# A hybrid S5 / HGRN2 / gated-MLP block in fp32: another order of the first twelve weight steps, and the S5 column work on GpSimd

## The chip, the cores and the metric

The kernel runs on one core of one Trainium2 chip. The metric is the device time of one execution in microseconds (us). Before the change it is 1422.86 us, the median of three runs (1422.52 to 1424.83). Lower is better.

## The reference

One block of a decoder in float32 on a sequence of 256 tokens with 2048 channels. `x` is normalised, multiplied by a wide input matrix, split into an S5 branch, an HGRN2 branch and two gates, merged, multiplied by an output matrix, added to `x`, and put through a gated MLP with a short causal convolution and a final norm.

```python
h = _rmsnorm(x, ln_mix_g[l])
proj = h @ w_in[l]                                  # 2048 x 9216
u_s5, q_h, f_h, i_h, g_h, gate_s5, gate_hgrn = jnp.split(proj, _in_splits(), axis=-1)
y_s5 = _s5_branch(u_s5, ...) @ w_proj_s5[l]
y_hgrn = _hgrn2_branch(q_h, f_h, i_h, g_h, lb_all[l], hgrn_norm_g[l]) @ w_proj_hgrn[l]
merged = sigmoid(gate_s5) * y_s5 + sigmoid(gate_hgrn) * y_hgrn
x = x + merged @ w_out[l]
x = x + _conv_glu_ffn(_rmsnorm(x, ln_ffn_g[l]), w_up[l], conv_w[l], conv_b[l], w_down[l])
# inside _s5_branch, per group g and state p (64 x 64 pairs):
dt = exp(log_dt)[:, None]; mag = exp(lam_re * dt)
abar_re = mag * cos(lam_im * dt); abar_im = mag * sin(lam_im * dt)
den = lam_re * lam_re + lam_im * lam_im
coef_re = ((abar_re - 1) * lam_re + abar_im * lam_im) / den
coef_im = (abar_im * lam_re - (abar_re - 1) * lam_im) / den
```

## The kernel before, in words

**Weight steps.** All weights are read once, in pieces of 128 x 1024 floats (512 KB). A piece is a step: SyncE's queue loads it into `wr` (four buffers), ScalarE (ACT) rounds it to `wh` (fp32r), VectorE (DVE) makes the rest `wl = wr - wh`, both with three buffers, and TensorE (PE) multiplies: for the feature-major jobs of the front (`fm_job`, wide) 8 matmuls of 512 columns with `wh` (against the high and the low half of x at once) and 8 of 256 columns with `wl`. A job is a block of 256 output columns: four steps (g = 0 to 3, one for each 512 rows of `w_in`) that add up in one PSUM bank, then an epilogue. The loop at the end of the kernel loads five steps ahead (`LOAD_AHEAD`) and splits two ahead (`LA`). Step i can run only when chunk g of x is ready: `x_chunk(g)` transposes 512 columns of x on PE (eight 128 x 128 transposes into `ax`), ACT writes the high half of `hT`, DVE the low half.

**The front.** Here jobs run one after the other: the first job (`u_jobs[0]`, four steps) needs all four chunks of x, and `between` puts `x_chunk(i+1)` between the two parts of step i. `warm_up` runs matmuls of `ones` into `dummy`. `x_norm` (sum of squares on DVE, then `rstd_of`, then `broadcast_rows` through PE) and `x_params` (a transpose of parameter rows to `colA`) follow at step 2. The epilogue `epi_u` of a job waits for the row `R_x` that `x_norm` makes.

**The sides.** `side_s5` and `side_hgrn` are generators that are advanced a few yields after each step (`side_run`), whenever the counted DVE load isn't ahead of PE's. The first part of `side_s5` is column work: parameters transposed to `colB` and `colC`, then some 110 small DVE operations on 128 x 32 or 128 x 16 floats (`exp_parts` for dt, for mag and for the softmax of the HGRN lower bound; a range reduction of the angle; the coefficients). Then come tables of angles (`tabA`, `tabB`), `BB` (coefficients times B), `X` (C placed by group, then transposed), and from there per channel tile `angle_sum` on GpSimd (128 x 1024), `b_place` into `zmat`, projections and scans.

**What sets the order.** The code gives an order, but a scheduler under it places each engine's instructions, and may put a later one ahead where it takes an engine for free; `tc.issue_after` (`behind_x`) keeps some from being put too early. Inside `tc.manual_schedule` (used by the changed kernel) the named engines keep the order of the code for what is written there; instructions written behind that block may still be placed between those of the block.

Of the kernel before, what the change touches and what calls it, by code (L numbers as in the profile page):

```python
# [110 lines left out]
def kernel(  # L111
# [28 lines left out]
    WARM_H = 6  # L140
    NORM_AT = 2
# [35 lines left out]
    ones = cst.tile([P, P], F32, name="ones")  # L177
    G.memset(ones, 1.0)
    epsc = cst.tile([P, 1], F32, name="epsc")
    G.memset(epsc, EPS)  # L180
# [17 lines left out]
    S.dma_start(out=packG, in_=rows(ln_mix_g))  # L198
    G.memset(packA, 0.0)
    ldt = pack[0:64, 5 * P:5 * P + 2]  # L200

    def load_params():
        S.dma_start(out=packA[16:32, :], in_=rows(lb_logits))
        S.dma_start(out=packA[56:72, :], in_=rows(ln_ffn_g))
        S.dma_start(out=packA[72:104, :], in_=a_re.rearrange("o (q g) p -> (o q) (g p)", g=2))
        S.dma_start(out=packB[0:32, :], in_=a_im.rearrange("o (q g) p -> (o q) (g p)", g=2))

# [63 lines left out]
    def fm_job(wap, c0, nkc, xs, epi, need=None, extra_load=None, wide=False):  # L271
# [121 lines left out]
    def x_chunk(g, between=None):  # L393

        for h in range(2):
            if h == 1 and between is not None:
                between()
# [5 lines left out]
            for a in range(2):  # L403
                kc = 4 * g + 2 * h + a
                A.activation(out=hT[:, kc, 0, :], in_=ax[:, a * T:(a + 1) * T], func=AF.Copy, scale=g_mix[:, kc:kc + 1])  # L405
# [5 lines left out]
        box["x"] = [getattr(i, "ins", i) for i in (last, lastp)]  # L411

    @contextmanager
    def behind_x():

        with tc.issue_after(box["x"][0]), tc.issue_after(box["x"][1]):
            yield

    def x_first():
        ax = axbank()  # L420
        PE.transpose(ax[:, 0:16], packG, ident[:16, :16])
        V.tensor_copy(g_mix, ax[:, 0:16])
        x_chunk(0, lambda: split_step(steps[0]))
        with behind_x():
            warm_up(WARM_H, ones)

    def x_norm():
        ss = cst.tile([P, 2, 4], F32, name="ss_x")
        for g in range(4):
            for j in range(2):  # L430
                xc = x_tok[j][g // 2][:, (g % 2) * 512:(g % 2) * 512 + 512]
                junk = tmp()
                V.scalar_tensor_tensor(out=junk, in0=xc, scalar=1.0, in1=xc, op0=ALU.mult, op1=ALU.mult,
                                       accum_out=ss[:, j, g:g + 1])
# [3 lines left out]
        broadcast_rows(R_x, r_x)  # L438
# [92 lines left out]
    u_jobs = [fm_job(w_in, 256 * p, 16, xs_hw, epi_u(p), wide=True) for p in range(4)]  # L531
# [25 lines left out]

    def exp_parts(new, xin):
# [6 lines left out]
        V.tensor_scalar(out=xc, in0=xin, scalar1=-88.0, scalar2=88.3, op0=ALU.max, op1=ALU.min)  # L565
        V.tensor_scalar(out=n, in0=xc, scalar1=1.4426950408889634, scalar2=ROUND, op0=ALU.mult, op1=ALU.add)
        V.tensor_scalar(out=n, in0=n, scalar1=-ROUND, scalar2=None, op0=ALU.add)
        V.scalar_tensor_tensor(out=r, in0=n, scalar=-0.693359375, in1=xc, op0=ALU.mult, op1=ALU.add)
        V.scalar_tensor_tensor(out=r, in0=n, scalar=2.12194440e-4, in1=r, op0=ALU.mult, op1=ALU.add)
        V.tensor_scalar(out=t, in0=r, scalar1=1.9875691500e-4, scalar2=1.3981999507e-3, op0=ALU.mult, op1=ALU.add)  # L570
        for c in (8.3334519073e-3, 4.1665795894e-2, 1.6666665459e-1, 5.0000001201e-1):
            V.tensor_tensor(out=t, in0=t, in1=r, op=ALU.mult)
            V.tensor_scalar(out=t, in0=t, scalar1=c, scalar2=None, op0=ALU.add)
        V.tensor_tensor(out=t, in0=t, in1=r, op=ALU.mult)
        V.tensor_tensor(out=t, in0=t, in1=r, op=ALU.mult)
        V.tensor_tensor(out=e, in0=t, in1=r, op=ALU.add)
        V.tensor_scalar(out=si, in0=n, scalar1=127.0, scalar2=8388608.0, op0=ALU.add, op1=ALU.mult)
        return e, si.bitcast(F32)

    def side_s5():  # L580
# [56 lines left out]
        V.tensor_scalar(out=t1, in0=th, scalar1=4097.0, scalar2=None, op0=ALU.mult)  # L637
        V.tensor_tensor(out=thh, in0=t1, in1=th, op=ALU.subtract)
        V.tensor_tensor(out=thh, in0=t1, in1=thh, op=ALU.subtract)
        V.tensor_tensor(out=thl, in0=th, in1=thh, op=ALU.subtract)  # L640
        for i, (src, c) in enumerate(((thh, c1), (thh, c2), (thl, c1))):
            V.tensor_scalar(out=ph, in0=src, scalar1=c, scalar2=None, op0=ALU.mult)
            V.tensor_scalar(out=pr, in0=ph, scalar1=ROUND, scalar2=ROUND, op0=ALU.add, op1=ALU.subtract)
            V.tensor_tensor(out=ph, in0=ph, in1=pr, op=ALU.subtract)
            V.tensor_scalar(out=pr, in0=ph, scalar1=ROUND12, scalar2=ROUND12, op0=ALU.add, op1=ALU.subtract)
            if i == 0:
                V.tensor_copy(hi, pr)
                V.tensor_tensor(out=lo, in0=ph, in1=pr, op=ALU.subtract)
            else:
                V.tensor_tensor(out=hi, in0=hi, in1=pr, op=ALU.add)  # L650
                V.tensor_tensor(out=ph, in0=ph, in1=pr, op=ALU.subtract)
                V.tensor_tensor(out=lo, in0=lo, in1=ph, op=ALU.add)
        V.scalar_tensor_tensor(out=lo, in0=thl, scalar=c2, in1=lo, op0=ALU.mult, op1=ALU.add)
        V.scalar_tensor_tensor(out=lo, in0=th, scalar=c3, in1=lo, op0=ALU.mult, op1=ALU.add)
        V.tensor_scalar(out=pr, in0=hi, scalar1=ROUND, scalar2=ROUND, op0=ALU.add, op1=ALU.subtract)
        V.tensor_tensor(out=hi, in0=hi, in1=pr, op=ALU.subtract)
# [3 lines left out]
        V.tensor_tensor(out=ph, in0=hi, in1=lo, op=ALU.add)  # L660
        V.tensor_scalar(out=pr, in0=ph, scalar1=-0.5, scalar2=0.5, op0=ALU.max, op1=ALU.min)
# [742 lines left out]
```

## Time and profile before

| | us |
|---|---|
| median of the runs shown | 1422.86 |
| the profiled execution's own time | 1422.75 |
| its span (first to last instruction) | 1420.6 |
| PE busy | 1403.4 |
| DVE busy | 1056.9 |
| ACT busy | 757.7 |
| GpSimd (POOL) busy | 38.0 |

In the timeline a row reads: start in us, length in us, engine, line, operation, tiles out<-in, shape, count, and in brackets how long the engine stood idle before it and what it waited for. Nearly every operation of PE and DVE goes through a metering helper, so it bears line L106; tiles tell them apart. A length can overlap the next start: the pace of PE is read from start to start. `PEld` are weight loads of PE, `SPq`, `ACTq` and `POOL DMA` rows are the issue of transfers.

### The profile page before, as it was taken

How to read it: one execution, taken by the hardware profiler on the slowest of the kernel's cores; microseconds unless marked ns; L12 is line 12 of the kernel's file. 1: busy time of each engine (PE TensorE's matmuls, PEld its weight loads, DVE VectorE, ACT ScalarE, POOL GpSimd, SP SyncE). 2: the span in 40 equal slices, each digit the busy share in tenths (PEclk: the TensorE clock that was granted, in tenths of full speed). 3: DMA queues.
4: the chain of work that ended last, by engine and by line, in shares of the span. 5: the costliest groups of instructions: out<-in, count | busy, mean ns of one | idle time of the engine just before them, and what ended most of it. 6: DMA issues, size and time to landing. Idle time of an engine off the chain costs nothing.

```text
span 1420.6 us, 20722 instructions
## 1 busy us (share of the span) xinstructions
PE 1403.4 (99%) x8008; PEld 1182.1 (83%) x8008; DVE 1056.9 (74%) x1453; ACT 757.7 (53%) x962; POOL 38.0 (3%) x33
## 2 busy tenths in 40 slices
PE   9999999999999999999999999999999999999997
PEld 7878887877778787888888888888888888888885
DVE  7999989998978968655777777777777775545454
ACT  5455576665655464454555555555555554434343
POOL 1040000000001000000000000000000000000000
PEclk9999999999999999999999999999999999999999
DMA  7865767666767466666666666666666666666653
GB/s 237 219 195 149 218 206 219 202 205 187 210 191 262 154 199 207 220 212 207 193 191 185 188 192 187 186 191 191 185 189 191 188 187 193 201 193 201 194 194 125
DMA packets 215940, 278.58 MB, mean 196 GB/s; under 512 B 19938, under 2 KB 141042, under 8 KB 215841
## 3 DMA queue, kind: packets, MB, share of 16 engines
q1 hardware_dynamic: 198496, 266.57, 60.5%
q10 hardware_dynamic: 17088, 10.49, 2.4%
q8 instruction: 63, 1.03, 0.3%
q14 instruction: 37, 0.30, 0.1%
q0 software_dynamic: 256, 0.19, 0.0%
HBM read 266.73 MB, written 10.49 MB: 195 GB/s over the span
## 4 chain that ended last, share of the span: by engine, by line
PE 95%; DVE 2%; DMA 1%; ACT 1%; issue 0%; POOL 0%; ACTq 0%; DVEq 0%; POOLq 0%
PE mm L106 87%; PE ax L106 7%; DVE u L106 1%; PE bu L106 1%; DMA u<-d 1%; DVE wl L106 1%; DMA u<-in_s_log_dt_dram 0%; ACT wh L256 0%; DVE t L106 0%; PE dummy L106 0%; DVE zmat L106 0%; ACT u L1275 0%; DVE x2g L106 0%; ACT hT L405 0%; ACT t L1259 0%
## 5 line engine op out<-in xcount | busy, mean ns | idle before, releaser
L256 ACT CAST wh<-wr 128x1024 fp32r<-128x1024 f32 x480 | 503.0, 1051 | 587.7 <-PE mm L106 424.2
L106 DVE TENSOR_TENSOR wl<-wr,wh 128x1024 fp32r<-128x1024 f32 x480 | 588.2, 1228 | 304.3 <-ACT wh L256 301.3
L106 PE MATMUL mm<-x2g,wh 128*128 128x512 f32 x1408 | 352.6, 392 | 0.0
L106 PEld LDWEIGHTS mm<-x2g,wh 128*128 128x128 f32 x1408 | 253.3, 189 | 45.3
L106 PE MATMUL mm<-wh,u 128*128 128x512 f32 x1040 | 260.7, 392 | 0.0
L106 PEld LDWEIGHTS mm<-wh,u 128*128 128x128 f32 x1040 | 193.7, 188 | 39.7
L106 PEld LDWEIGHTS mm<-x2g,wl 128*128 128x128 f32 x1408 | 192.0, 190 | 13.6
L106 PE MATMUL mm<-x2g,wl 128*128 128x256 f32 x1408 | 196.4, 282 | 0.0
L106 PE MATMUL mm<-wh,hT 128*128 128x512 f32 x768 | 193.6, 394 | 0.0
L106 PEld LDWEIGHTS mm<-wh,hT 128*128 128x128 f32 x768 | 142.1, 188 | 33.5 <-issue 2.9
L106 PE MATMUL mm<-wl,u 128*128 128x512 f32 x520 | 140.6, 390 | 0.0
L106 DVE TENSOR_TENSOR u<-u,u 128x512 f32<-128x512 f32 (+4 forms) x144 | 114.8, 821 | 0.5
L106 PEld LDWEIGHTS mm<-wl,u 128*128 128x128 f32 x520 | 97.4, 188 | 20.0
L106 PE MATMUL mm<-wl,hT 128*128 128x512 f32 x384 | 102.9, 390 | 0.0
L106 PE MATMUL mm<-hT,wh 128*128 128x512 f32 x384 | 100.4, 401 | 0.8 <-ACT wh L256 0.8
L106 PEld LDWEIGHTS mm<-wl,hT 128*128 128x128 f32 x384 | 72.1, 188 | 15.5
L106 PEld LDWEIGHTS mm<-hT,wh 128*128 128x128 f32 x384 | 69.9, 192 | 14.8 <-ACT wh L256 1.0
L106 DVE SCALAR_TENSOR_TENSOR t<-ub,colC,t 128x256 f32<-128x256 f32 x176 | 73.3, 479 | 0.0
L106 PEld LDWEIGHTS mm<-hT,wl 128*128 128x128 f32 x384 | 52.1, 191 | 4.7 <-DVE wl L106 1.3
L106 PE MATMUL mm<-hT,wl 128*128 128x256 f32 x384 | 54.3, 284 | 0.3 <-DVE wl L106 0.3
L1200 ACT ACTIVATE t<-ub,colC 128x256 f32<-128x256 f32 x88 | 48.0, 593 | 0.0
L106 PE MATMUL ax<-wh,u 128*128 128x512 f32 x176 | 43.3, 389 | 0.0
(186 smaller groups left out, 861.2 us busy)
## 6 DMA issues: line engine op xcount, KB each, us to landing
wr<-in_w_up_dram SPq DMA_DIRECT2D x176, 512.0 KB, 4.5
wr<-in_w_in_dram SPq DMA_DIRECT2D x144, 512.0 KB, 4.4
wr<-in_w_down_dram SPq DMA_DIRECT2D x88, 512.0 KB, 4.7
wr<-in_w_out_dram SPq DMA_DIRECT2D x32, 512.0 KB, 4.2
wr<-in_w_proj_s_dram SPq DMA_DIRECT2D x16, 512.0 KB, 4.0
wr<-in_w_proj_hgrn_dram SPq DMA_DIRECT2D x16, 512.0 KB, 4.8
d<-t ACTq DMA_DIRECT2D x28, 256.0 KB, 4.4
rl<-d SPq DMA_DIRECT2D x16, 256.0 KB, 4.3
```

The costliest lines, as they stand in the source:

```text
L106: return fn(*args, **kw)
L256: A.copy(st.wh, st.w)
L1200: A.activation(out=av, in_=ub[:, a, 0:T], func=AF.Identity, scale=conv_col(0, n), bias=colC[:, 264 + n:265 + n])
```

## The change

It reorders the front: the first three jobs go chunk by chunk (`FRONT = 3`; steps 0, 1, 2 use chunk 0 of x, steps 3, 4, 5 chunk 1, and so on; the third job gets the PSUM bank `bu`, named `mf` here), under a hand-written order for SyncE, PE, ACT and DVE. The first weight piece and the first chunk of x come in halves on two queues. Squares of x go from DVE to ACT. The S5 column work goes from DVE to GpSimd (`E = G`; a fused multiply-add becomes two instructions), the softmax part behind `BB`. Four parameter loads go from SyncE's queue to GpSimd's. The diff, cut:

```diff
-    WARM_H = 6
-    NORM_AT = 2
+    WARM_H = 3
+    FRONT = 3
...
-    G.memset(ones, 1.0)
+    V.memset(ones, 1.0)
...
-    S.dma_start(out=cf, in_=cst_f)
+    A.dma_start(out=cf, in_=cst_f)
...
-    def load_params():
-        S.dma_start(out=packA[16:32, :], in_=rows(lb_logits))
...
+    G.dma_start(out=packA[72:104, :], in_=a_re.rearrange("o (q g) p -> (o q) (g p)", g=2))
+    G.dma_start(out=packB[0:32, :], in_=a_im.rearrange("o (q g) p -> (o q) (g p)", g=2))
+    G.dma_start(out=packA[16:32, :], in_=rows(lb_logits))
+    G.dma_start(out=packA[56:72, :], in_=rows(ln_ffn_g))
...
+                if fine and g == 0:
+                    for h, part in ((0, 0), (0, 1), (0, 2), (1, 0), (1, 1), (1, 2)):
+                        for k in (2 * h, 2 * h + 1):
+                            for j in range(2):
...
+                                PE.matmul(o, (wl if part == 2 else wh)[:, k, cols], hT[:, k, part % 2, :],
+                                          start=k == 0 and part == 0, stop=False)
+                    return
...
+    def load_first():
...
+        for h in range(2):
+            for j in range(2):
+                S.dma_start(out=x_tok[j][0][:, h * T:(h + 1) * T], in_=x[0, j * P:(j + 1) * P, h * T:(h + 1) * T])
+            st.dma = A.dma_start(out=v3(st.w, 4)[:, 2 * h:2 * h + 2, :], in_=st.src[:, 2 * h:2 * h + 2, :])
...
+    def x_squares(g):
+        for j in range(2):
...
+            A.activation(out=junk, in_=xc, func=AF.Square, accum_out=ss_x[:, j, g:g + 1])
...
+    steps[:4 * FRONT] = [steps[4 * p + g] for g in range(4) for p in range(FRONT)]
...
+    E = G
+    def fused(out, in0, scalar, in1, op0, op1, t):
+        E.tensor_scalar(out=t, in0=in0, scalar1=scalar, scalar2=None, op0=op0)
+        E.tensor_tensor(out=out, in0=t, in1=in1, op=op1)
...
+        yield ("step", 9)
         A.activation(out=sn, in_=pr, func=AF.Sin, scale=TWO_PI)
...
+        E.tensor_tensor(out=den, in0=den, in1=t1, op=ALU.add)
...
+        yield ("step", 11)
+        V.reciprocal(out=den, in_=den)
+        E.tensor_tensor(out=cr, in0=nr, in1=lam_re, op=ALU.mult)
...
+        yield ("step", 18)
+        V.reciprocal(out=e1, in_=e0)
...
+    with tc.manual_schedule(engines={ET.SP, ET.PE, ET.Activation, ET.DVE}):
+        load_first()
+        table_up()
+        for i in range(1, LOAD_AHEAD):
+            load_front(i)
+        warm_up(WARM, ones)
+        x_first()
+        for i in range(4 * FRONT):
+            g, r = divmod(i, FRONT)
+            load_front(i + LOAD_AHEAD)
+            if r == FRONT - 1 and g < 3:
+                x_chunk(g + 1)
+            split_step(steps[i + 1])
...
+            work(i, steps[i])
+            if i == 3 * FRONT - 1:
+                x_norm()
+            elif i == 3 * FRONT + 1:
+                broadcast_rows(R_x, r_x)
+            if i == 2:
+                x_params()
+            if i >= 2:
...
+                side_run()
```

How it moves instructions, at three places. First PE at the start of the program, before the change (`ax` are transposes, `u_88` to `u_91` the tiles of x, `mm_225` the bank of the first job, `wh_196` and `wl_197` the two parts of step 0, `wh_215` of step 1, `wh_221` of step 2):

```order
L106 MATMUL dummy<-ones 128x128 x6
L106 MATMUL ax_234<-cf,u_88 128x128
L106 MATMUL mm_225<-hT,wh_196 128x512 x8
...
L106 MATMUL mm_225<-hT,wl_197 128x256 x8
L106 MATMUL mm_225<-hT,wh_215 128x512 x2
L106 MATMUL ax_274<-cf,u_89 128x128
...
L106 MATMUL mm_225<-hT,wl_216 128x256 x8
```

The same place after the change (`u_90` to `u_93` are now x; `mm_226`, `mm_259` and `mf_304` the banks of the first three jobs, `u_78` the parameter rows):

```order
L106 MATMUL dummy<-ones 128x128 x3
L106 MATMUL mm_226<-hT,wh_186 128x256 x8
L106 MATMUL mm_226<-hT,wl_187 128x256 x4
...
L106 MATMUL mm_259<-hT,wh_218 128x512 x8
L106 MATMUL mm_259<-hT,wl_219 128x256 x8
...
L106 MATMUL mf_304<-hT,wl_256 128x256 x8
L106 MATMUL ax_321<-cf,u_78 128x104
L106 MATMUL ax_331<-cf,u_78 128x64
L106 MATMUL ax_334<-cf,u_78 128x128 x2
L106 MATMUL ax_334<-cf,u_78 128x96
L106 MATMUL mm_226<-hT,wh_296 128x512 x8
```

Chunk 1 of x was needed right after step 0 and is now needed after step 2; the parameter transposes moved from steps 7 and 8 to the place between steps 2 and 3.

Second, DVE behind the split of step 3 (`wl_297`), after the change; `wl_368` and `wl_449` are the splits of steps 4 and 5, `u_413` holds small S5 columns, here `den`, and the brackets name the semaphore that a row waits for:

```order
L106 TENSOR_TENSOR wl_297<-wr_175,wh_296 128x1024 [waits DMAHW4_49,Activation_49]
L106 COPY colA<-ax_321 128x104 [waits PE_49]
L106 COPY u_78<-u_78 32x128 [waits DMASW7_49]
L106 COPY colB<-ax_331 128x64 [waits PE_49]
L106 COPY colC<-ax_334 128x352 [waits PE_49]
L106 RECIPROCAL u_413<-u_413 128x32 [waits Pool_49]
L106 TENSOR_TENSOR wl_368<-wr_177,wh_367 128x1024 [waits DMAHW5_49,Activation_49]
L106 TENSOR_TENSOR wl_449<-wr_216,wh_448 128x1024 [waits DMAHW6_49,Activation_49]
```

The reciprocal of `den` is written behind step 11, and stands behind the split of step 3, ahead of the splits of steps 4 and 5; before the change no DVE row of the front waits for GpSimd.

Third, GpSimd at the start of the column work, after the change (`u_339` and `u_413` hold the columns):

```order
L655 TENSOR_SCALAR u_339<-colA 128x32 [waits DVE_49]
L616 TENSOR_SCALAR u_339<-colB 128x32 [waits DVE_49]
L706 TENSOR_TENSOR u_413<-u_339 128x32 [waits Pool_49]
L617 TENSOR_SCALAR u_339<-u_339 128x32 [waits Pool_49]
L618 TENSOR_SCALAR u_339<-u_339 128x32 [waits Pool_49]
...
L678 TENSOR_SCALAR u_413<-u_413 128x32 [waits Pool_49]
L708 TENSOR_TENSOR u_413<-u_413 128x32 [waits Pool_49]
```

These rows stood on DVE before; the last one makes `den`. From the row that reads `colB` to that last row there are 40 instructions, and nearly all of them wait for an earlier one of the same engine.

More of the change, by code (lines that the diff above doesn't have):

```diff
@@ L174, in at, with rows @@
             return self.units[k // 4][:, (k % 4) * T:(k % 4 + n) * T]
+    pack = unit()
+    packA, packB = pack[0:104, 0:P], pack[0:64, P:2 * P]
+    packC = [pack[0:P if i < 2 else 96, (2 + i) * P:(3 + i) * P] for i in range(3)]
+    def rows(ap):
+        return ap.rearrange("o (r c) -> (o r) c", c=P)
+    packG = pack[0:16, 6 * P:7 * P]
+    S.dma_start(out=packG, in_=rows(ln_mix_g))
     ones = cst.tile([P, P], F32, name="ones")
-    G.memset(ones, 1.0)
+    V.memset(ones, 1.0)
     epsc = cst.tile([P, 1], F32, name="epsc")
@@ L410, in x_chunk @@
                                               op0=ALU.mult, op1=ALU.subtract)
-        box["x"] = [getattr(i, "ins", i) for i in (last, lastp)]
+        box["x"] = [getattr(i, "ins", i) for i in (last, lastp, lasta)]
     @contextmanager
     def behind_x():
-        with tc.issue_after(box["x"][0]), tc.issue_after(box["x"][1]):
+        with tc.issue_after(box["x"][0]), tc.issue_after(box["x"][1]), tc.issue_after(box["x"][2]):
             yield
     def x_first():
+        st = steps[0]
+        uid[0] += 1
+        st.wh = wp.tile([P, 1024], F32R, tag="wh", name=f"wh{uid[0]}", bufs=LA + 1)
+        st.wl = wp.tile([P, 1024], F32R, tag="wl", name=f"wl{uid[0]}", bufs=LA + 1)
         ax = axbank()
@@ L422, in x_first @@
         V.tensor_copy(g_mix, ax[:, 0:16])
-        x_chunk(0, lambda: split_step(steps[0]))
-        with behind_x():
-            warm_up(WARM_H, ones)
-    def x_norm():
[L428 to L434, printed above, removed]
+        for h in range(2):
+            ax = axbank()
+            half = slice(h * 512, h * 512 + 512)
+            A.copy(st.wh[:, half], st.w[:, half])
+            for a in range(2):
+                for j in range(2):
+                    c = (2 * h + a) * P
+                    PE.transpose(ax[:, a * T + j * P:a * T + (j + 1) * P], x_tok[j][0][:, c:c + P], ident)
+            for a in range(2):
+                kc = 2 * h + a
+                xa, gk = ax[:, a * T:(a + 1) * T], g_mix[:, kc:kc + 1]
+                if kc == 0:
+                    V.tensor_scalar(out=hT[:, kc, 0, :], in0=xa, scalar1=gk, scalar2=None, op0=ALU.mult)
+                else:
+                    A.activation(out=hT[:, kc, 0, :], in_=xa, func=AF.Copy, scale=gk)
+            for a in range(2):
+                kc = 2 * h + a
+                V.scalar_tensor_tensor(out=hT[:, kc, 1, :], in0=ax[:, a * T:(a + 1) * T], scalar=g_mix[:, kc:kc + 1],
+                                       in1=hT[:, kc, 0, :].bitcast(F32), op0=ALU.mult, op1=ALU.subtract)
+            V.tensor_tensor(out=st.wl[:, half], in0=st.w[:, half], in1=st.wh[:, half].bitcast(F32), op=ALU.subtract)
+        warm_up(WARM_H, ones)
+    ss_x = cst.tile([P, 2, 4], F32, name="ss_x")
+    def x_squares(g):
+        for j in range(2):
+            xc = x_tok[j][g // 2][:, (g % 2) * 512:(g % 2) * 512 + 512]
+            junk = tmp()
+            A.activation(out=junk, in_=xc, func=AF.Square, accum_out=ss_x[:, j, g:g + 1])
+    def x_norm():
+        ss = ss_x
         ssum = cst.tile([P, 2], F32, name="ssum_x")
@@ L529, with front_bank @@
     gh_dram = [[scratch() for _ in range(2)] for _ in range(4)]
-    u_jobs = [fm_job(w_in, 256 * p, 16, xs_hw, epi_u(p), wide=True) for p in range(4)]
+    def front_bank():
+        uid[0] += 1
+        return psb.tile([P, 2, 512], F32, tag="bu", name=f"mf{uid[0]}")
+    u_jobs = [fm_job(w_in, 256 * p, 16, xs_hw, epi_u(p), wide=True, bank=front_bank if p == 2 else mm_bank, fine=p == 0)
+              for p in range(4)]
+    steps[:4 * FRONT] = [steps[4 * p + g] for g in range(4) for p in range(FRONT)]
     for p in range(4):
@@ L685, in side_s5 @@
+        fused(nr, cm1, 1.0, em1, ALU.add, ALU.mult, nr)
+        E.tensor_tensor(out=nr, in0=nr, in1=cm1, op=ALU.add)
+        E.tensor_tensor(out=ni, in0=mag_c, in1=sn, op=ALU.mult)
+        E.tensor_tensor(out=den, in0=lam_re, in1=lam_re, op=ALU.mult)
+        E.tensor_tensor(out=t1, in0=lam_im, in1=lam_im, op=ALU.mult)
+        E.tensor_tensor(out=den, in0=den, in1=t1, op=ALU.add)
         AB = unit()
@@ L695, in side_s5 @@
             yield
+        yield ("step", 11)
+        V.reciprocal(out=den, in_=den)
+        E.tensor_tensor(out=cr, in0=nr, in1=lam_re, op=ALU.mult)
+        E.tensor_tensor(out=t1, in0=ni, in1=lam_im, op=ALU.mult)
+        E.tensor_tensor(out=cr, in0=cr, in1=t1, op=ALU.add)
+        E.tensor_tensor(out=cr, in0=cr, in1=den, op=ALU.mult)
+        E.tensor_tensor(out=ci, in0=ni, in1=lam_re, op=ALU.mult)
+        E.tensor_tensor(out=t1, in0=nr, in1=lam_im, op=ALU.mult)
+        E.tensor_tensor(out=ci, in0=ci, in1=t1, op=ALU.subtract)
+        E.tensor_tensor(out=ci, in0=ci, in1=den, op=ALU.mult)
+        yield ("step", 12)
         BB = unit()
@@ L876, in side_hgrn @@
         mraw = reload_tile()
-        S.dma_start(out=mraw[:, 0:112], in_=cst_m)
-        V.tensor_copy(masks, v3(mraw[:, 0:80], 5))
+        with behind_x(), tc.issue_after(getattr(steps[4 * FRONT].dma, "ins", steps[4 * FRONT].dma)):
+            S.dma_start(out=mraw[:, 0:112], in_=cst_m)
+            V.tensor_copy(masks, v3(mraw[:, 0:80], 5))
         q, k, f = (Chunks(8) for _ in range(3))
@@ L1326, in side_run, with load_front, work @@
                     return
-    for i in range(LOAD_AHEAD):
-        if i < 4:
-            load_x_chunk(i)
+    def load_front(i):
+        if i % FRONT == 0 and i < 4 * FRONT:
+            load_x_chunk(i // FRONT)
         load_step(steps[i])
-        if i == 4:
-            load_params()
-    table_up()
-    warm_up(WARM, ones)
-    x_first()
-    for i in range(1, LA):
-        split_step(steps[i])
-    for i in range(3):
-        steps[i].between = lambda i=i: x_chunk(i + 1)
-    load["dve"] = load["pe"] = 0.0
-    for i, st in enumerate(steps):
-        if i + LOAD_AHEAD < len(steps):
-            load_step(steps[i + LOAD_AHEAD])
-        if i + LA < len(steps):
-            split_step(steps[i + LA])
+    def work(i, st):
         run_later(i=i)
@@ L1356 @@
             st.extra_load()
+        fin.add(("step", i))
         st.mm(st)
-        if i == NORM_AT:
-            with behind_x():
-                x_norm()
-                x_params()
         if st.after is not None:
             job, fn = st.after
-            later.append((i + 1, job, fn))
-        load["dve"] = max(load["dve"], load["pe"] - 4.0)
-        if i >= S5_START:
-            pauses[0] = 0
-            if i == S5_START:
-                with behind_x():
-                    side_run()
-            else:
-                side_run()
+            later.append((i + (2 if i < 4 * FRONT else 1), job, fn))
+    ET = mybir.EngineType
+    with tc.manual_schedule(engines={ET.SP, ET.PE, ET.Activation, ET.DVE}):
+        load["dve"] = load["pe"] = 0.0
+        load_first()
[10 more added lines that the diff above has]
+            split_step(steps[i + 1])
+            if i == 0:
+                x_squares(0)
+            elif r == FRONT - 1 and g < 3:
+                x_squares(g + 1)
+            work(i, steps[i])
[6 more added lines that the diff above has]
+            if i >= 2:
+                pauses[0] = 0
+                load["dve"] = max(load["dve"], load["pe"] - 4.0)
+                side_run()
+    for i in range(1, LA):
+        split_step(steps[4 * FRONT + i])
+    for i, st in enumerate(steps):
+        if i < 4 * FRONT:
+            continue
+        if i + LOAD_AHEAD < len(steps):
+            load_front(i + LOAD_AHEAD)
+        if i + LA < len(steps):
+            split_step(steps[i + LA])
+        work(i, st)
+        load["dve"] = max(load["dve"], load["pe"] - 4.0)
+        pauses[0] = 0
+        side_run()
     run_later(i=len(steps) + 10)
```

157 lines of the change are left out of this document (65 added, 92 removed).

## The prediction

> **What bounds the kernel now.** The page first: span, busy times and the chain that ended last; then who waited for whom on PE.
>
> ```profile
> span 1420.6 us, 20722 instructions
> PE 1403.4 (99%) x8008; PEld 1182.1 (83%) x8008; DVE 1056.9 (74%) x1453; ACT 757.7 (53%) x962; POOL 38.0 (3%) x33
> PE 95%; DVE 2%; DMA 1%; ACT 1%; issue 0%; POOL 0%; ACTq 0%; DVEq 0%; POOLq 0%
> PE ax L106 <- DVE u L106: 3.3, 2, 2.3
> PE ax L106 <- DMA u<-in_x_dram: 1.1, 1, 1.1
> PE mm L106 <- ACT wh L256: 0.8, 1, 0.8
> ```
>
> PE is busy for 99% and is 95% of the chain. The change takes no matmul away, so it can only win what PE loses, and PE's waits are a few us in all. Everything is therefore decided by when PE starts on weights, and by the few places of the first 110 us where it stands. The timeline of PE and DVE shows both.
>
> ```profile
> 1.00 3.36 PE L106 MATMUL dummy<-ones 128*128 128x128 f32 x14 [1.00 <-POOL epsc L180]
> 5.67 0.48 PE L106 MATMUL ax<-cf,u 128*128 128x128 f32 x1 [1.10 <-DMA u<-in_x_dram]
> 8.26 2.43 PE L106 MATMUL dummy<-ones 128*128 128x128 f32 x12
> 10.56 1.62 PE L106 MATMUL mm<-hT,wh 128*128 128x512 f32 x6
> 47.07 2.12 PE L106 MATMUL mm<-hT,wh 128*128 128x512 f32 x8 [0.78 <-ACT wh L256]
> 49.97 2.00 PE L106 MATMUL mm<-hT,wh 128*128 128x512 f32 x8
> 51.81 1.12 PE L106 MATMUL mm<-hT,wl 128*128 128x256 f32 x8
> 52.77 2.00 PE L106 MATMUL mm<-hT,wh 128*128 128x512 f32 x8
> 95.34 1.03 PE L106 MATMUL ax<-cf,u 128*128 128x128 f32 x8
> 96.14 2.09 PE L106 MATMUL mm<-hT,wh 128*128 128x512 f32 x8
> 101.50 1.14 PE L106 MATMUL ax<-cf,u 128*128 128x128 f32 x8 [2.33 <-DVE u L106]
> 102.32 3.67 PE L106 MATMUL mm<-hT,wh 128*128 128x512 f32 x8
> 102.00:106.00 4.00, 4.00 (x16) 3.29 (x14) 2.41 (x3) 2.66 (x4) 0.00 (x0) 0.57 0.75 222
> ```
>
> Weights start at 10.56. A step takes 2.80 us (49.97 to 52.77): 1.84 for the wide part, 0.96 for the rest. Steps 0 to 11 fill 10.56 to 49.97, 39.4 us: twelve times 2.80 is 33.6, the 24 transposes of chunks 1 to 3 are 2.4 (eight take 0.80, from 95.34 to 96.14), and parameter and broadcast matmuls about 1.6 (below); so only 1.8 us are waits. The other loss is at 99 to 106: 2.33 us idle, and then eight wide matmuls in 3.67 instead of 2.00, since the granted clock is 0.57 in that window. That is 4.0 us together.
>
> **The change part by part. Start.** Two rows of the windows (the last number is GB/s):
>
> ```profile
> 0.00:5.00 5.00, 3.57 (x15) 3.24 (x15) 0.15 (x1) 1.49 (x2) 4.25 (x16) 1.00 0.37 100
> 5.00:10.00 5.00, 4.03 (x17) 3.45 (x18) 1.89 (x6) 2.14 (x5) 1.20 (x6) 1.00 0.98 335
> ```
>
> 0.5 MB is in by 5 us and then 0.335 MB per us. I keep that curve: the first halves of x and of weight piece 0 with the constants are 0.6 MB, in at 5.3; the second halves end at 1.1 MB, 6.8 us. Then come four transposes and three dummies of two passes, all at the early pace of about 0.21 us (14 passes in 3.36, 12 in 2.43): 0.85 and 1.3, so weights start near 9.0 instead of 10.56: **-1.55**. PE runs at the slow pace until about 10 (the 12 passes from 8.26), so step 0 gets **+0.5**, and 24 narrow matmuls of 0.12 instead of 8 wide and 8 narrow are **+0.1**. Pieces 1 and 2 (1.6 and 2.2 MB: 8.3 and 10) and chunk 1 (2.7 MB, 11.5) come before PE wants them, since three steps per chunk are 8.4 us of PE work; the waits of 1.8 go: **-1.8**. The moved loads cost nothing: SyncE's queue has four issues less, and GpSimd's twelve at some 0.5 us are out by 8 us, ten before `ax_321`. Squares on ACT (eight) lie beside a PE step each; ACT is 53% busy. What covers them is the two steps by which splits run ahead.
>
> **Parameters.** PE now does these three transposes in a row, and the second waits for two DVE copies.
>
> ```profile
> 36.03 0.63 PE L106 MATMUL ax<-dg,ones 128*128 128x128 f32 x4
> 36.51 0.28 PE L106 MATMUL ax<-cf,u 104*128 104x104 f32 x1
> 37.87 0.46 PE L106 MATMUL ax<-cf,u 128*128 128x128 f32 x3
> 37.04 0.26 DVE L106 COPY colA<-ax 128x104 f32<-128x104 f32 x1
> 5.70 0.45 DVE L106 COPY u<-u 32x128 f32<-32x128 f32 x1 [3.27 <-DMA u<-in_s_log_dt_dram]
> ```
>
> 0.26 and 0.45 less some overlap: **+0.6**. The front without the reciprocal is then -1.55 + 0.5 + 0.1 - 1.8 + 0.6 = **-2.1**.
>
> **The reciprocal on DVE.** In the new order DVE takes `den`'s reciprocal ahead of the split of step 4, and `den` is the end of 40 GpSimd instructions that begin when `colB` is copied. Behind the waiting reciprocal stand the splits of steps 4 and 5 and the low halves of chunk 2, and PE waits for the first. From the copy of `colB` PE still has the last parameter transposes (0.5), step 3 (2.80) and the wide part of step 4 (1.84), together 5.1. DVE needs the copy and hand-over (0.4), 40 GpSimd instructions of c each, the reciprocal (0.34), the split (1.22) and hand-overs (0.2). PE stands 40c - 3.0. No row shows c: GpSimd did no small arithmetic before. The nearest rows:
>
> ```profile
> L180 POOL MEMSET epsc<- 128x1 f32 x1 | 0.1, 99 | 0.0
> L732 POOL MEMSET zmat<- 128x256 f32 x1 | 0.3, 331 | 0.0
> L741 POOL TENSOR_TENSOR u<-u x8: 1942/2544/7529, 77.8 to 285.3; 128x1024 f32<-128x1024 f32 x8
> 1413.52 0.16 DVE L106 TENSOR_TENSOR fin<-fin 128x1 f32<-128x1 f32 x1
> 1413.71 0.16 DVE L106 TENSOR_TENSOR fin<-fin,fin 128x1 f32<-128x1 f32 x1
> 57.74 0.34 DVE L106 RECIPROCAL u<-u 128x32 f32<-128x32 f32 x1
> L106 DVE TENSOR_TENSOR wl<-wr,wh 128x1024 fp32r<-128x1024 f32 x480 | 588.2, 1228 | 304.3 <-ACT wh L256 301.3
> ```
>
> The memsets give 0.10 + 0.0009 per element: 0.13 for 32, the low end, as nothing is read there. On DVE a chain in which each waits for the last advances by 0.19 (1413.52 to 1413.71). From above: if the sum of 1024 elements in 1.94 to 2.1 us spends two thirds to all of its time on elements, 0 to 0.7 is fixed; half of that, 0.35, plus a wait gives 0.40 as high end. I take **0.25**: nearer in size to the memsets, in kind to the sums, and above DVE's 0.19. 40c is then 10.0 (5.2 to 16), and PE stands **+7.0** (2.2 to 13). PE idle for 2.33 us was followed by the half clock, so **+1.7** again. After it DVE has 1.2 to 1.8 us of work per PE step of 2.8 and catches up. ACT's two sines wait for the 84th of these instructions; at c = 0.25 that is 21 us after `colB`, beside steps 4 to 9 and the stall.
>
> **Later.** The 4.0 us at 99 to 106 came from DVE running late:
>
> ```profile
> 77.83 11.68 POOL L741 TENSOR_TENSOR u<-u 128x1024 f32<-128x1024 f32 x3 [71.63 <-DVE u L106]
> 82.88 0.68 DVE L106 TENSOR_TENSOR u<-u,u 128x512 f32<-128x512 f32 x1
> 83.48 4.25 DVE L106 TENSOR_SCALAR u<-u,cf 128x512 f32<-128x512 f32 x2
> 95.32 5.24 DVE L106 TENSOR_TENSOR wl<-wr,wh 128x1024 fp32r<-128x1024 f32 x3 [0.59 <-ACT wh L256]
> 100.48 0.87 DVE L106 TENSOR_SCALAR u<-u,cf 128x512 f32<-128x512 f32 x2
> L106 DVE TENSOR_TENSOR u<-u 128x32 f32<-128x32 f32 x34 | 5.7, 185 | 0.1
> L106 DVE TENSOR_SCALAR u<-u 128x32 f32<-128x32 f32 x28 | 4.8, 176 | 0.1
> ```
>
> Two scalings took 4.25 beside GpSimd's sums, and 0.87 alone. Some 100 small operations leave DVE (the last two rows, of 40 to 72 us: 62 of them take 10.5 us), which speaks for no gap; a second reciprocal, of 8 columns, waits for 25 GpSimd instructions, and the sums still run beside the same scalings, which speaks for one. I take half back: **-2.0** (-4.0 to +4.0).
>
> By the Trainium skill's "SBUF — State Buffer", SBUF: two separate sides, DVE with two SBUF inputs and GpSimd exclude each other on a shared port pair; the trace agrees, as the first sum, issued at 77.83, ended 2 us after DVE's two-input run to 83.56. By that rule the chain of 40 runs free while DVE stands at the reciprocal.
>
> **Sum.** Against the profiled execution's own 1422.75 us (its span 1420.6 and 2.15 around it; 0.1 below the median): -2.1 + 7.0 + 1.7 - 2.0 = +4.6, so 1427.4.
>
> **Rivals.** *Cheap instructions (faster):* c is 0.13 as the memsets say. PE stands 2.2 us, the clock holds, and the later gap goes: -2.1 + 2.2 - 4.0 = -3.9, 1418.9. For it: nothing of 32 elements need take long. Against it: a chain of waits costs DVE 0.19 a link. The change turns at about c = 0.18 (-2.1 + 4.2 + 1.7 - 4.0). *No change:* c at DVE's 0.19: 4.6 + 1.7 - 2.1 - 4.0 = +0.2, 1423.0; with half the gap 1425. *First use:* the longest sum took 7.53, 5.4 over the plain 2.11, and it was GpSimd's first arithmetic. If that is a price of the first use and not DVE's run, the chain begins 5.4 later: 1427.4 + 5.4 = 1432.8. For it: it was the first; against: DVE's run of two-input operations to 83.56 accounts for it, with 1.9 left. The Trainium skill's "GPSIMD Engine Reference", 2.1 Instruction dispatch, tells of about 6 us for loading code at the first call; the one row here can't tell it from the port. *It doesn't do what it says:* early data comes no sooner, so the first -1.55 is lost; 1429, inside the forecast's range.
>
> **Chances.** Forecast 0.47, cheap 0.16, no change 0.25, first use 0.12. Faster by over 0.2% (under 1420.0; a measurement of this kernel tells about that much) 0.16, within it 0.25, slower 0.59. The range goes from the cheap case at 1419 to beyond first use at 1435, which takes in c = 0.40 (1433.4); dearer and cheaper chains are the 2 in 10 left out. The forecast's own range is 1424 to 1433.
>
> **What would show it.** Right: weights near 9.0 on PE; DVE idle before its 128 x 32 reciprocal, released by GpSimd, near 30 us; PE waiting some 7 us for `wl` after one wide part; a clock of 0.5 behind it; step 12 about 4 to 7 us late against 49.97. GpSimd's small rows give c by start to start. Wrong: that reciprocal not waiting, or PE standing elsewhere; weights starting at 10 or later would void the first term; no gap near 100 would make the last -4.0.

## The result, and the profile after

| | median us | lowest to highest, runs | ratio to before, 95% interval |
|---|---|---|---|
| before | 1422.69 | 1421.39 to 1424.83, 4 | |
| after | 1441.95 | 1440.53 to 1443.73, 4 | 1.0135, 1.0117 to 1.0152 |

The changed kernel is slower by 19 us. The profiled execution took 1443.73 us, its span is 1441.6 against 1420.6: 21.0 us to find. First the page of the changed kernel (span, busy times, chain that ended last), then the list of what PE waited for (us in total, times, longest).

```profile
span 1441.6 us, 20726 instructions
PE 1407.4 (98%) x8010; PEld 1187.7 (82%) x8010; DVE 1043.4 (72%) x1327; ACT 762.2 (53%) x978; POOL 77.8 (5%) x162
PE 92%; DVE 4%; POOL 1%; issue 1%; DMA 1%; ACT 0%; SPq 0%; DVEq 0%
```

```profile
PE ax L106 <- DVE u L106: 7.3, 2, 7.1
PE mm L106 <- DVE wl L106: 6.4, 2, 6.1
PE mm L106 <- DVE t L106: 3.8, 1, 3.8
PE mm L106 <- ACT wh L254: 2.9, 1, 2.9
```

These four lines make 20.4 us, where before had 3.3 (for `u`), 0.8 (`wh`) and 0.3 (`wl`): 16.0 more. PE's own busy time grew by 4.0 (1407.4 against 1403.4) with two instructions more. Together that is 20.0 of the 21.0. So nearly the whole loss lies in PE standing at four places and working slowly behind them. The timeline of the changed kernel's PE shows where, and the windows show the granted clock there (the number behind ACT's and POOL's, third from the right).

```profile
9.80 2.05 PE L106 MATMUL mm<-hT,wh 128*128 128x256 f32 x8
27.93 2.66 PE L106 MATMUL mm<-hT,wh 128*128 128x512 f32 x8 [2.87 <-ACT wh L254]
36.67 2.08 PE L106 MATMUL mm<-hT,wl 128*128 128x256 f32 x8 [6.08 <-DVE wl L106]
61.44 3.78 PE L106 MATMUL mm<-hT,wh 128*128 128x512 f32 x8 [3.75 <-DVE t L106]
106.14 1.94 PE L106 MATMUL ax<-cf,u 128*128 128x128 f32 x8 [7.05 <-DVE u L106]
107.73 3.69 PE L106 MATMUL mm<-hT,wh 128*128 128x512 f32 x8
```

```profile
28.00:40.00 12.00, 5.92 (x25) 4.88 (x26) 2.62 (x3) 1.19 (x2) 10.24 (x34) 0.57 0.30 79
106.00:112.00 6.00, 5.86 (x23) 5.15 (x24) 2.68 (x3) 3.06 (x5) 0.00 (x0) 0.57 0.39 118
```

Eight wide matmuls take 2.0 at full clock; at 61.44 and 107.73 they take 3.7. Now the engines that PE waits for, in the timeline of the changed kernel: two reciprocals on DVE and the row that empties a PSUM bank, GpSimd's first rows, the 40th and 84th instruction of its column work from `colB` on and the one behind them, and ACT with its queue.

```profile
35.19 0.35 DVE L106 RECIPROCAL u<-u 128x32 f32<-128x32 f32 x1 [12.38 <-POOL u L708]
55.50 0.69 DVE L106 TENSOR_TENSOR u<-cf,u 128x512 f32<-128x512 f32 x1
60.70 0.68 DVE L106 TENSOR_TENSOR t<-mm,t 128x512 f32<-128x512 f32 x1
92.82 0.20 DVE L106 RECIPROCAL u<-u 128x8 f32<-128x8 f32 x1 [6.13 <-POOL u L759]
21.30 0.31 POOL L655 TENSOR_SCALAR u<-colA 128x32 f32<-128x32 f32 x1 [10.53 <-DVE colA L106]
22.14 0.32 POOL L616 TENSOR_SCALAR u<-colB 128x32 f32<-128x32 f32 x1 [0.54 <-DVE colB L106]
34.91 0.25 POOL L708 TENSOR_TENSOR u<-u 128x32 f32<-128x32 f32 x1
51.70 1.18 POOL L696 TENSOR_SCALAR u<-u 128x32 f32<-128x32 f32 x1
55.95 0.35 POOL L705 TENSOR_TENSOR u<-mag,u 128x32 f32<-128x32 f32 x1 [3.07 <-ACT u L699]
18.31 4.68 ACTq L636 DMA_DIRECT2D u<-in_s_b_im_dram  x1
23.03 3.13 ACTq L638 DMA_DIRECT2D u<-in_s_c_re_dram  x1
26.84 2.00 ACT L254 CAST wh<-wr 128x1024 fp32r<-128x1024 f32 x2 [5.84 <-issue]
54.34 1.28 ACT L699 ACT_TABLE_LOAD   x1
58.73 1.06 ACT L485 COPY t<-mm 128x512 f32<-128x512 f32 x2
```

From 22.14 to the end of L708 at 35.16, 40 instructions: c is 13.0 / 40 = **0.325**. L696 is the 84th, and it ends at 52.88. ACT's queue issues the loads of B and C ahead of the split of step 4, and the issues take 4.68 and 3.13 us: that is the wait for `wh`.

The wait for `t` at 61.44 is no wait for GpSimd. PE needs a PSUM bank that ACT's copy at 58.73 and then DVE's `t<-mm,t` at 60.70 empty. ACT comes to the two sines, which need the 84th instruction, at 54.34 (the row there is the load of their table), 1.5 us after it has ended; GpSimd waits 3.07 us for ACT there, not ACT for GpSimd. DVE does not pause either: from 55.50 to 60.70 it works through eight operations of the angle tables, which the hand-written order puts ahead of `t<-mm,t`.

### The profile page after: what moved, and what is told of

It is laid out like the page before. It is cut to its first block, busy times and chain, and to the rows that moved or that the text cites. A ratio compares the mean times of both kernels' runs of the same rounds, so it can differ in the third digit from the quotient of the medians.

```text
span 1441.6 us, 20726 instructions
## 1 busy us (share of the span) xinstructions
PE 1407.4 (98%) x8010; PEld 1187.7 (82%) x8010; DVE 1043.4 (72%) x1327; ACT 762.2 (53%) x978; POOL 77.8 (5%) x162
## 4 chain that ended last, share of the span: by engine, by line
PE 92%; DVE 4%; POOL 1%; issue 1%; DMA 1%; ACT 0%; SPq 0%; DVEq 0%
PE mm L106 83%; PE ax L106 7%; DVE u L106 2%; DVE wl L106 1%; PE bu L106 1%; DMA u<-d 1%; PE mf L106 1%; DMA u<-in_x_dram 0%; DVE t L106 0%; POOL u L606 0%; POOL u L624 0%; ACT wh L254 0%; POOL u L623 0%; POOL u L616 0%; POOL u L607 0%
## 5 line engine op out<-in xcount | busy, mean ns | idle before, releaser
L106 DVE TENSOR_TENSOR wl<-wr,wh 128x1024 fp32r<-128x1024 f32 (+1 forms) x481 | 593.7, 1237 | 304.2 <-ACT wh L254 301.2
L106 DVE TENSOR_TENSOR u<-u,u 128x512 f32<-128x512 f32 (+3 forms) x140 | 111.9, 824 | 0.3
L106 PE MATMUL mm<-hT,wh 128*128 128x512 f32 (+1 forms) x360 | 94.3, 406 | 6.6 <-DVE t L106 3.8
L106 PEld LDWEIGHTS mm<-hT,wh 128*128 128x128 f32 x360 | 66.9, 199 | 19.7 <-DVE t L106 4.0
L106 PEld LDWEIGHTS mm<-hT,wl 128*128 128x128 f32 x352 | 49.1, 195 | 10.2 <-DVE wl L106 7.0
L106 PE MATMUL mm<-hT,wl 128*128 128x256 f32 x352 | 50.4, 287 | 6.1 <-DVE wl L106 6.1
```

What stands on the lines that cost most here:

```text
L106: return fn(*args, **kw)
```

## The experiments

**Theory 1**: the two reciprocals at the head of DVE's queue cost the time. **Theory 2**: the end of GpSimd's chain costs it, whoever stands there. **A third**: the new order of the front does. In the first four kernels one reciprocal or both are held back behind the newest split (`box_s["wl"]` is that instruction), and in both_sp the loads are moved too. Added lines shift the line numbers of these kernels by a few.

```diff
# den
-        V.reciprocal(out=den, in_=den)
+        with tc.issue_after(box_s["wl"]):
+            V.reciprocal(out=den, in_=den)
# e1: with the two operations behind it, from ahead of the first angle sums to behind them
+        with tc.issue_after(box_s["wl"]):
+            V.reciprocal(out=e1, in_=e0)
# both: den and e1.  both_sp: both, and the four loads of B and C
-            A.dma_start(out=v3(dst, 32), in_=src.rearrange("o (q g) p c -> (o g p) q c", g=2))
+            S.dma_start(out=v3(dst, 32), in_=src.rearrange("o (q g) p c -> (o g p) q c", g=2))
```

den. 

> Only den's reciprocal is held back on DVE, behind a split that DVE does about step 14; everything else is as changed. Theory 1 (the reciprocals at the head of DVE's queue cost the time, by the wait and the half clock behind it): PE's wait of 6.08 us for wl at 30.6 goes and with it the half pace up to 39.5 (some 1.4 us): 1441.95 - 7.5 = 1434.4, with the waits at 25, 57.5 and 99 where they were. Theory 2 (it is GpSimd's slow chain of column work whoever waits for it): the wait turns up later, where the tables of angles or the coefficients need the chain, and the time stays within 3 us of 1441.95.

e1. 

> Only the second reciprocal (8 columns, softmax of the lower bound) is moved behind the first two angle sums in the code and held back on DVE; den's stays where the change put it. Theory 1: DVE's idle 6.13 us ending at 92.8 goes, so the scalings of u end some 6 us sooner, PE's wait of 7.05 us at 99 shrinks to 1 to 2.5 us, and at under about 2 us the half clock behind it (3.4 us) goes too: 1433 to 1437. Theory 2 (GpSimd's angle sums beside DVE set that wait): it stays above 5 us and the time within 3 us of 1441.95.

both. 

> Both reciprocals held back. Theory 1: the two gains add up, 1441.95 - 7.5 - 7 = about 1427, still over the kernel before by the waits at 25 (2.87 for wh) and 57.5 (3.75 for a PSUM bank) with their half clocks. Theory 2: above 1438. A third theory, that the new order of the front costs time by itself, would show as a time above 1427 without any of these waits.

both_sp. 

> As both, and the four loads of B and C leave ACT's queue for SyncE's. If ACT's issue of them (3.1 us for one) is what made wh late at 25, the wait of 2.87 us goes with the slow step behind it (0.7 us): 3 to 4 us under both. If something else made wh late, no difference over 1 us.

Measured: den 1441.88 (ratio 1.0127), e1 1439.62 (1.0108), both 1433.71 (1.0074), both_sp 1434.21 (1.0075). Alone, holding `den` back gains nothing, although its wait is gone. PE's timeline says why, in den and in both_sp:

```profile
59.42 3.78 PE L106 MATMUL mm<-hT,wh 128*128 128x512 f32 x8 [8.73 <-DVE t L106]
```

```profile
58.84 3.78 PE L106 MATMUL mm<-hT,wh 128*128 128x512 f32 x8 [13.85 <-DVE t L106]
53.92 0.23 ACT L702 ACTIVATE u<-u 128x32 f32<-128x32 f32 x1 [11.24 <-POOL u L699]
```

The wait that went at 30 us came back at 50. In both_sp, where the wait for `wh` is gone too, PE stands once, for 13.85 us, and goes on at 58.84 instead of 61.44. Its 84th GpSimd instruction releases the sine at 53.9; in the changed kernel it ended at 52.88. What stands there is ACT's sine (11.24 us idle; 5.88 in den, none in the changed kernel), with the copy that empties the bank behind it, and the tables on DVE. In the changed kernel the reciprocal had held DVE and PE up for so long that the chain was over when ACT and DVE came to these; without that stand PE asks for the bank sooner (at 50.7 us in den, at 57.7 in the changed kernel), and the chain's end decides. That is theory 2 for the first chain: the gains that theory 1 gave den and both_sp did not come, though each took its own wait away. For the second reciprocal theory 1 holds in part: in e1 PE's wait at 99 fell from 7.05 to 2.50 us. both gains 8.2 us, more than den and e1 apart (0.1 and 2.3), and lies between the times of the two theories (1427, and over 1438): no wait of over 1.3 us is left near 100 in it, where e1 keeps one of 2.50 with half pace behind it. Why DVE gets there sooner in both was not traced.

In the next two kernels nothing on ACT or DVE stands at the first chain. held: the sines and the ten operations of the tables come after step 12 and behind the newest splits. held_sp: after step 14, on top of both_sp.

```diff
-        yield ("step", 9)
-        A.activation(out=sn, in_=pr, func=AF.Sin, scale=TWO_PI)
+        yield ("step", 12)
+        with tc.issue_after(box_s["wh"]):
+            A.activation(out=sn, in_=pr, func=AF.Sin, scale=TWO_PI)
...
+            with tc.issue_after(box_s["wl"]):
                 V.tensor_tensor(out=dst, in0=io, in1=hi.unsqueeze(2).to_broadcast([P, 32, 16]), op=ALU.mult)
```

held. 

> As both, and the two sines on ACT and the ten table operations on DVE, which need the end of GpSimd's first 84 instructions, are emitted after step 12 and held behind the splits there, so that nothing on ACT's or DVE's queue stands at GpSimd's chain before 50 us. If the chain's end at 51 us, and whoever stands at it, is the cost (theory 2 as the four runs left it: the wait moved from 30 to 50 us and cost 8.9 us there), PE's wait of 8.73 us at 50.5 and the half pace behind it (3.4 us) go: 1433.7 - 12 = about 1421.5, with the wait for wh at 24 left. Rival: the new order of the front costs by itself; then over 1428 without a wait of over 4 us.

held_sp. 

> As held, with sines and tables after step 14 instead of 12, and B's and C's loads on SyncE's queue: the wait of 3.2 us for wh at 24 goes too, with about 1 us of half pace: 4 us under held, 1417 to 1418, faster than before. If the chain still reaches PE, a wait for wl shows near 50 us and the gain over held is under 2 us.

Measured: held 1429.5 (1.0043), held_sp 1426.77 (1.0023, 1.0014 to 1.0033). The wait for `t` is gone in both, and in held_sp the one for `wh` at 24 too; from 8 to 62 us PE waits only some 0.2 us at a time, but for 1.00 at the parameter transposes. I had expected 8 to 9 us more of a gain: a new wait shows near 97, this time of `bu` for `u`, which ACT writes behind the angle sums, and one for `wh` at 93 (PE's waits in held_sp). held moves both the operations that stood at the chain and the tables' own work out of the way of the epilogue, so by itself it does not tell these two apart; den's idle times and dve do.

```profile
PE bu L106 <- ACT u L262: 3.2, 1, 3.2
PE mm L106 <- ACT wh L254: 2.0, 1, 2.0
```

Two kernels take the parts of the change apart. g_only is the kernel before with `E = G` (and each fused multiply-add as two instructions) and nothing else; dve is the changed kernel with the column work on DVE; front_only is dve with the S5 part begun only behind the hand-written block.

```diff
# dve
-    E = G
+    E = V
# front_only: dve, and in the loop over the first twelve steps
-            if i >= 2:
-                pauses[0] = 0
-                load["dve"] = max(load["dve"], load["pe"] - 4.0)
-                side_run()
```

g_only. 

> The kernel before with its old front, and only the column work moved to GpSimd (E = G, as in the change; both reciprocals stay on DVE in the scheduler's order). If GpSimd's chain behind a reciprocal on DVE is the cost, this alone is slower than before: two chains share GpSimd, the softmax reciprocal stands some 50 x 0.33 = 16 us behind them, splits run two steps (5.6 us) ahead: PE stands about 8 us near 60, with a half clock behind it: 1432 to 1438. If the front is the cost, it is within 3 us of 1423.

dve. 

> The changed kernel with the column work back on DVE (E = V, fused operations as before), the rest of the change kept, so that the hand-written order now puts some 60 small operations of 0.19 us (11 us) ahead of the splits of steps 4 and 5. If GpSimd's slow chain is the cost, this is faster than the changed kernel by 5 us or more (no stand at 57 and 99; at 24 to 40 the wait for wh and about 5 us for wl stay): 1428 to 1435. If the front's order is the cost, it is 1440 or more.

front_only. 

> The new front alone: column work on DVE with the fused operations of before, and the S5 part begun only behind the hand-written block, at step 12, in the scheduler's order. If the front costs nothing by itself, PE shows no wait over 1.1 us from 10 to 50 us, step 12 starts 0.8 us ahead of before (49.2), and the time is 1420 to 1424 depending on the gap near 100, which may move as the column work begins 3 us later than before. If the front's order is a cost, 1428 or more.

Measured: g_only 1452.07 (1.0201), dve 1441.7 (1.0128), front_only 1433.42 (1.0081). PE's waits in g_only, and two rows of its DVE timeline; then PE's waits in dve, and PE's timeline in front_only:

```profile
PE mm L106 <- DVE wl L106: 22.2, 3, 10.7
```

```profile
56.23 0.20 DVE L106 RECIPROCAL u<-u 128x8 f32<-128x8 f32 x1 [13.84 <-POOL u L617]
72.46 1.33 DVE L106 TENSOR_TENSOR u<-cf,u 128x512 f32<-128x512 f32 x2 [9.85 <-POOL u L662]
```

```profile
PE mm L106 <- DVE t L106: 5.7, 1, 5.7
PE mm L106 <- ACT wh L254: 5.4, 1, 5.4
PE mf L106 <- DVE wl L106: 4.0, 1, 4.0
```

```profile
7.85 1.20 PE L106 MATMUL mm<-hT,wh 128*128 128x256 f32 x8
44.73 2.00 PE L106 MATMUL mm<-hT,wh 128*128 128x512 f32 x8
546.97 1.96 PE L106 MATMUL ax<-cf,u 128*128 128x128 f32 x7 [5.20 <-DVE u L106]
```

The column work on GpSimd costs 28 us in the old front, 14 to 20 more than I expected: there too DVE stands at the softmax reciprocal, and then, which I had not counted, at the tables, with splits behind each. dve was a miss: it ties with the changed kernel. The hand-written order puts the column work ahead of the splits of steps 4 and 5 and the tables ahead of the epilogue, and DVE's own operations there cost PE 4.0 us for `wl` and 5.7 for `t`, where the changed kernel has 6.1 and 3.8; the 5.4 for `wh` are again ACT's issues of B's and C's loads (5.74 and 4.25 us on its queue). So the place in DVE's and ACT's order decides, not the engine alone. The front by itself does what it should: in front_only step 12 stands at 44.73 (49.97 before; the `colB` and `colC` transposes come after it here, before it in the kernel before). But its S5 part begins later (`colB` is copied at 47.9 us, 21.8 in the changed kernel), and from step 12 to its end the kernel takes 15.7 us longer than the one before, 5.20 of it in one wait at 541, where before has none of that size. A time over 1428 was to speak for the front as the cost; it doesn't, since PE's timeline has no wait from 8 to 50 us and the loss comes behind the front. That the late S5 part causes it is likely, not shown.

The last five kernels ask what is left between 80 and 104 us. sm_late moves the softmax chain of 25 GpSimd instructions behind the first two angle sums; sm_late2 also takes its first maximum (on DVE) early; sm_early puts it behind the 84th instruction; sm_mid keeps it ahead of the sums, with the early maximum; mid_late is sm_mid with the first projection `bu` five yields later. All stand on held_sp.

```diff
# sm_late2 (sm_late without the first line); sm_mid has box_s["ci"], behind the coefficients
+        V.tensor_tensor(out=m, in0=l0, in1=l1, op=ALU.max)
         yield ("step", 14)
...
+        with tc.issue_after(box_s["as"]):
+            E.tensor_tensor(out=z[:, 0:8], in0=l0, in1=m, op=ALU.subtract)
...
# mid_late
         b_trans(0)
         yield
+        yield
+        yield
+        yield
+        yield
         bu = b_proj(0, 0)
```

sm_late. 

> As held_sp, with the softmax chain of 25 GpSimd instructions (8.3 us at 0.33) moved in the code from ahead of the first angle sums to behind them. If that chain, which stands ahead of the sums on GpSimd's queue, is what makes PE wait at 93 to 104 (about 8 us lost there), the sums end some 8 us sooner and that loss falls to 2 us or less: 1426.8 - 6 = about 1421. If the sums themselves beside DVE are the cost, the loss stays: within 2 us of 1426.8.

sm_early. 

> As held_sp, with the softmax chain put directly behind the 84th GpSimd instruction, where GpSimd stands idle for the sines in part, and its reciprocal where it was. The coefficient chain then ends some 6 us later (76 instead of 70) on GpSimd, beside DVE's tables and splits; the angle sums some 8 us sooner than in held_sp. Same cause as sm_late: about 1421; if the later coefficients make DVE's reciprocal of den stand (behind it a split), a wait of 3 to 5 us for wl near 72 shows instead, and 1425 to 1428.

sm_late2. 

> As sm_late, with the maximum ahead of the softmax chain taken early on DVE, so that the 25 GpSimd instructions follow the two angle sums at 76 us at once and end near 84, ten us before DVE reaches their reciprocal. If that reciprocal's wait (5.49 us of DVE, 2.98 us of PE at 100.2 and the half clock behind it) is what keeps sm_late over the kernel before, 5 to 6 us go: 1419 to 1420, faster than before by 0.2 to 0.3%. If the chain on GpSimd slows DVE's work at 76 to 84 instead, the wait of 2.5 us at 81 grows and 1423 or more results.

sm_mid. 

> As held_sp, with the maximum ahead of the softmax chain taken early on DVE, so that the 25 GpSimd instructions run at 70.8 to 79 us, where GpSimd stood idle for that maximum until 78.4, and the angle sums end near 84 instead of 92. If GpSimd standing idle and then blocking is what costs held_sp its 8 us at 93 to 104, the wait for the tables (3.2 us) and the half clock go: 1426.8 - 6 = 1421 or less. If it is the angle sums beside DVE, wherever they run, as sm_late2 (sums at 71, wait of 2.6 us at 81) lets one think, a wait of about 2.5 us near 85 takes its place: 1423 to 1425.

mid_late. 

> As sm_mid, with the first projection of the S5 part (bu on PE) emitted five yields later, so that PE reaches it 12 matmul groups (about 5 us) after sm_mid did. If the two waits of sm_mid at 94 and 99 (3.18 us for ACT's u and 1.96 for DVE's u) and the half clock behind them (1.5 us) are only PE asking too early, they go and nothing later needs the S5 part sooner: 1422.7 - 6 = 1416 to 1418, faster than before by 0.35 to 0.5%. If later steps do need it (as front_only, whose S5 part began 27 us late, lost 5 us at one later place), the time stays at 1421 or more.

Measured: sm_late 1425.13 (1.0013), sm_early 1428.5 (1.0039), sm_late2 1424.11 (1.0007, 0.9998 to 1.0016), sm_mid 1422.72 (0.9998, 0.9989 to 1.0007), mid_late 1424.61 (1.001, 1.0001 to 1.002). sm_late, sm_late2 and mid_late miss the times that their first branches gave (1421, 1419 to 1420, 1416 to 1418). In sm_early the later coefficients make PE wait 7.2 us for `wl` at 75, the second branch of its expectation, only dearer. sm_late2 has the sums at 71, beside DVE's products, and waits 2.6 us for `u` at 81; sm_mid has them at 87 and waits 3.2 for ACT's `u`, which is made from them, and 2.0 for DVE's (PE's waits in sm_mid). mid_late, meant to win some 6 us, loses the first of these two waits and keeps 1.70 of the second; its time did not fall (the profiled run, 1422.58, is among its faster ones).

```profile
PE bu L106 <- ACT u L262: 3.2, 1, 3.2
PE bu L106 <- DVE u L106: 2.0, 1, 2.0
```

No kernel here beats the one before. With every wait at a GpSimd chain taken away, column work on GpSimd and the new front give at best a tie (sm_mid and sm_late2, whose intervals take in 1). What is left of the gap near 100 was not settled.

## Why the prediction was wrong

The direction was right, the size was not: +4.6 forecast, +19.3 measured (the medians), outside the range. By its steps:

- **Front, -2.1: right as a sum.** PE's timeline in sm_late2, the same front with no wait at GpSimd:

```profile
9.01 1.62 PE L106 MATMUL mm<-hT,wh 128*128 128x256 f32 x8
48.02 2.00 PE L106 MATMUL mm<-hT,wh 128*128 128x512 f32 x8
```

  Weights start at 9.01 (forecast 9.0), and step 12 is 1.95 us ahead of 49.97. Of the 1.8 us that the sum calls waits, before's list of PE's waits has 0.78 behind 10.5 us; that the rest were waits is not shown. In the profiled run of the changed kernel weights start at 9.80, since the second halves of x kept PE waiting for 1.43 us.
- **The reciprocal, +7.0: the mechanism was right, c was mis-sized**: 0.325 instead of 0.25, within the bounds of 0.13 to 0.40. By the prediction's own 40c - 3.0 PE stands 10.0; it stood 6.08 for `wl` and, just before, 2.87 for `wh`, 8.95 together.
- **The step that failed** is the sentence behind the reciprocal, that DVE then "has 1.2 to 1.8 us of work per PE step of 2.8 and catches up", with the sines "beside steps 4 to 9 and the stall". Nothing was priced between the reciprocal and the gap near 100, and PE stood 3.75 us there and worked at half pace behind. DVE did not catch up: from 49.8 to 61.4 it was busy for 10.8 of 11.6 us, and the angle tables, 5.2 us of them ahead of the operation that empties the first job's bank, had no term. dve shows that no GpSimd chain is needed for this: with the column work on DVE the same stand is 5.65 us. The sines were covered in the changed kernel, though not by the margin that I gave: the 84th instruction ended 30.7 us behind `colB` (22.14 to 52.88), not 21. They were covered only because of the stand at the reciprocal: den takes that away, the sines then wait 5.88 us, and the time is the same.
- **ACT's issues** of B's and C's loads, which the change puts ahead of the split of step 4, had no term: 2.87 us.
- **Half clock, +1.7 once**: there were three such places where before had one, and PE's busy time grew by 4.0.
- **The gap near 100, -2.0 (-4.0 to +4.0)**, is the term that was furthest off: the wait there grew from 2.33 to 7.05 us, +4.7, past the upper bound before any clock. The second reciprocal, named in the prediction as what speaks for a gap, idled DVE for 6.13 us; e1, which moves it, has a wait of 2.50, about what before had.
- **Rivals.** Cheap and no change fall with c. First use falls by the row at 21.30: GpSimd's first arithmetic took 0.31 us. The Trainium skill's "GPSIMD Engine Reference", 2.1 Instruction dispatch, tells of about 6 us for loading code at a first call; no run here shows that, so of the two explanations weighed there for the 7.53 us sum of before, DVE's two-input run beside it is the one left. That early data come no sooner falls with 9.01 and 9.80 against 10.56.

## What to carry to other kernels

When work moves to a slower engine, write down every instruction of the in-order engines that needs any result of it, with when the result comes and what stands behind that instruction; here a wait taken away at the first of them came back at the next until the last one was late enough. Do the same for the instruction that empties a buffer: add up what stands ahead of it on its own engine. Count DMA issues as instructions of the queue that they stand on. Work that left DVE was worth nothing to this kernel, since PE had hardly waited for it.

## What the runs showed of the hardware

GpSimd's chain on 128 x 32 floats advanced by 0.325 us per instruction while DVE stood idle; DVE's on the same size advanced by 0.22 in dve (DVE's timeline, start to start):

```profile
21.00 0.18 DVE L106 TENSOR_SCALAR u<-u 128x32 f32<-128x32 f32 x1
21.22 0.19 DVE L106 TENSOR_TENSOR u<-u 128x32 f32<-128x32 f32 x1
```

The softmax chain took 8.9 us for 25 instructions in the changed kernel, where DVE was idle for the last 6.1 of them, and 16.6 us in sm_mid (POOL's timeline: first, a slow one and last), where DVE did splits and products of two inputs:

```profile
70.62 0.66 POOL L764 TENSOR_TENSOR u<-colA,u 128x8 f32<-128x8 f32 x1
79.87 1.18 POOL L627 TENSOR_TENSOR u<-u 128x16 f32<-128x16 f32 x1
87.06 0.20 POOL L768 TENSOR_TENSOR u<-u 128x8 f32<-128x8 f32 x1
```

The other way, beside the angle sums of sm_late2 DVE's product took 2.42 instead of 0.68 and its split 2.95 instead of 1.21 (DVE's timeline):

```profile
71.14 2.42 DVE L106 TENSOR_TENSOR t<-u,u 128x512 f32<-128x512 f32 x1
73.48 2.95 DVE L106 TENSOR_TENSOR wl<-wr,wh 128x1024 fp32r<-128x1024 f32 x1
```

Both fit what the Trainium skill's "SBUF — State Buffer", SBUF: two separate sides, says of the port pair that DVE with two inputs and GpSimd share. And a stand of PE is not always followed by the half clock: 2.33 us were in the kernel before, 2.52 us in sm_late were not (PE's timeline; eight wide matmuls in 1.93 from start to start):

```profile
83.52 1.09 PE L106 MATMUL ax<-cf,u 128*128 128x128 f32 x8 [2.52 <-DVE u L106]
84.36 2.09 PE L106 MATMUL mm<-hT,wh 128*128 128x512 f32 x8
86.29 1.11 PE L106 MATMUL mm<-hT,wl 128*128 128x256 f32 x8
```
